# Row sums behind the first query tile, low keys in both halves, head 1's first loads inside the list, adaptive bias behind its weights

## The chip, the cores and the metric

The kernel runs on one core of one Trainium2 chip. The time is the device time of one launch in microseconds (us). TensorE (PE, with its weight loads PEld) multiplies matrices, VectorE (DVE) and ScalarE (ACT) work on elements, GpSimd (POOL) and SyncE (SP) issue most of the transfers (DMA), POOL also a few element operations. SP and POOL hand out their transfers in order, each from a list of its own.

## The reference

One layer of a streaming encoder for 1024 prompt rows and 32 sample rows (1056 together), width 1024, all in fp32:

```python
ada = silu(c) @ w_ada + b_ada        # shift1, scale1, gate1, shift2, scale2, gate2
h = rms_norm(x, g_pre_mix) * (1 + sc1) + sh1
q_lat, c_kv, k_r, q_b, k_b, v_b, g_a, g_b = split(h @ w_in)
o_a = multi-head latent attention (8 heads, chunk mask, softmax)
o_b = stick-breaking attention of q_b, k_b, v_b (8 heads of 64, strictly causal):
    z  = q k / 8
    sp = where(mask, softplus(z), 0); later = reverse_cumsum(sp) - sp
    a  = where(mask, exp(log_sigmoid(z) - later), 0);  o = a v
merged = sigmoid(g_a) * (o_A @ w_proj_a) + sigmoid(g_b) * (o_B @ w_proj_b)
x = x + gt1 * rms_norm(merged @ w_out)
x = x + gt2 * rms_norm(conv_ffn(rms_norm(x) * (1 + sc2) + sh2))
```

The new keys and values of the stick-breaking branch are outputs too, in their natural layout.

## The kernel before

Every fp32 product is made of three products of shorter numbers: each operand is split in a high half (`hi`, ACT, line 65) and a low half (`lo`, DVE, line 68), and PE adds high·high, high·low and low·high. A tile's weights come into a `wr` buffer by DMA, ACT writes `wh`, DVE `wl`, and then PE can start.

**The stage that makes queries, keys and values** (`stage_qkv`) computes 16 column tiles of `h @ w_in` with 128 columns each. The first three are made plainly (`mtile`): the query tile of heads 0 and 1 (its spill of high and low halves to DRAM is issued on POOL), the key tile of the same heads, and a tile of the query latents (written to DRAM as `l2d`). The other ten are made in five pairs by `pair(i, ta, tb, ua, ub)`: a scheme with seven block products in place of eight, of which five, w1·T2, w2·T1, w3·T3, w4·T4 and w5·B22, work on sums. The sums on the weights' side (lines 575, 576, 579, 580) are made by DVE in each pair, and each is then split by ACT and DVE (`half`). The sums on the rows' side, `T1` to `T4`, are made once from the normalised rows `F12`, `F22` in `fq` by the generator `sums()`: its first step makes T3 and T2 on DVE and ACT, its second T1, its third T4. `next(S)` runs a step; it stands once behind the latent tile and twice inside `pair`. `fq` is later the place of the pairs' results `ua`, `ub`.

What belongs to a finished tile is deferred to `after(kind, p, u)`, and a step of it is run by each `bg()` in the next pairs: for keys and values PE transposes the tile (`natural`, line 456), ACT copies it to a `nat` buffer (462), POOL writes it out (468), and for values DVE splits it into an `sg` buffer (473, 474) that POOL spills as `vd` (475). For a query tile `after` splits at once: ACT writes QH into an `sg` buffer, POOL spills `qh`, DVE makes the low half in place (488), POOL spills `ql`. There are two `sg` buffers, shared by QH, KH and V.

**The attention stage** (`stage_sb`, with buffers from `att_pools`) goes over four pairs of heads (p = 0 to 3), in each over two heads, and for each head over eight query tiles of 128 rows, two to a group: groups 0 to 3 of the list are head 0's, 4 to 7 head 1's. A token such as `S2.0a` is a step (here the score), the group, the tile in it, and a part of the row. For a head, `queries(p, h)` loads on SP: Q high, KH into both halves of a 128-partition tile, Q low into the other half of Q, and the low keys into one half of `KLz`, whose other half is set to zero once by POOL (line 1084). `score` is then two matmuls: KH·Q (1098) and KLz·Q (1099). The V load follows (1094). These tiles lie where the sums T were, and the `att` buffers where `fq` and the `qkv` buffers were, so their first use waits for the last reader there.

The order on PE, ACT and DVE in this stage is a list written by hand, `ORDER` (line 657), which begins `S0.0 S0.1 a0.0 S1.0 a0.1 e0.0 e0.1 l0.0 f1 f1 l0.1 x0.0`: `S` a score tile, `a`, `e`, `l` absolute value, exponential and logarithm on ACT, `x`, `c`, `d` steps on DVE, `E` the last exponential, `T`, `h`, `v`, `V` transposes and values, and `f` a step of other work that fills PE. The filling work is `gates()`: the gate columns of `h @ w_in` (lines 72 to 74), and between them steps of `ada_step`, in which PE multiplies `w_ada` row blocks (line 211). For each block of columns `ada_step` issues four loads of `b_ada` (207), then the `w_ada` loads (209). `then` holds work that is issued after a token of the list, by name. SP has at most eight transfers under way: the next one waits for the landing of the one eight before it.

Of the kernel before, what the change touches and what calls it, by code (L numbers as in the profile page):

```python
# [8 lines left out]
F32 = mybir.dt.float32  # L9
# [8 lines left out]
P = 128  # L18
D = 1024
KT = 8  # L20
TP = 1024
# [11 lines left out]
BIG = 1056  # L33
# [11 lines left out]
class K:  # L45
# [151 lines left out]
    def ada_step(self, n, pool, tp, late):  # L197


        nc, a = self.nc, self.a  # L200
        ps = self.bank("mm")
        for i, (v, k) in enumerate(self.ada_todo[:n]):
            if k == 0:
                self.acc = self.tl(tp, [P, 256], F32, "ada")
                for j in range(4):
                    c = v * D + j * 256
                    nc.sync.dma_start(self.acc[32 * j : 32 * j + 32], a["b_ada"][0, c : c + 256].partition_broadcast(32))
            w = self.tl(pool, [P, D], F32, "wr")
            nc.sync.dma_start(w, a["w_ada"][0, k * P : (k + 1) * P, v * D : (v + 1) * D])
            for j in range(4):  # L210
                nc.tensor.matmul(ps[32 * j : 32 * j + 32, :256], self.cT[:, k], w[:, j * 256 : j * 256 + 256],
                                 start=i == 0, stop=i == n - 1)
            if i < n - 1:
                yield
        acc = self.acc
        late.append(lambda: nc.vector.tensor_tensor(acc, acc, ps[:, :256], ALU.add))
        del self.ada_todo[:n]
        self.ada_sum = v if k == KT - 1 else None
        yield
# [195 lines left out]
    def stage_qkv(self):  # L415
# [63 lines left out]
        def after(kind, p, u):  # L479

            x = u[:, :TP]
            low = x.bitcast(F32R)
            if kind == "q":
                QH = sg()
                self.hi(QH, x, 0.125)
                nc.gpsimd.tensor_scalar(self.qsb[:, p], u[:, TP:T], 0.125, None, ALU.mult)
                spill("qh", p, QH)
                stt(low, x, 0.125, fl(QH), ALU.mult, ALU.subtract)
                spill("ql", p, low)
                return  # L490
            if kind == "k":
                KH = sg()
                self.hi(KH, x)
                nc.gpsimd.tensor_copy(self.ksb[:, p], u[:, TP:T])
                spill("kh", p, KH)
            for t0 in (0, 4, 8):
                natural(u, p, kind, t0)
                yield
            if kind == "k":
                self.lo(low, x, KH)  # L500
                spill("kl", p, low)
# [59 lines left out]
        S = sums()  # L561

        def pair(i, ta, tb, ua, ub):

            def plus(u, h, b, ps, q):
                add(u[:, HC * h + cs[b].start : HC * h + cs[b].stop], ps[:, : ns[b]], q[:, cs[b]], ALU.add)

            ra, rb = raws.pop(0)
            a0, a1 = half(ra[:, :512]), half(ra[:, 512:])
            X, Y = ([self.bank(g) for _ in range(2)] for g in ("mm", "s"))  # L570
            for ps, w, x in ((X, a0, B11), (Y, a1, B21)):
                for b in range(2):
                    prod(ps[b], b, w, x, True)
            s1a, s1b = S1[:, :512], S1[:, 512:]
            add(s1b, rb[:, :512], rb[:, 512:], ALU.add)
            add(s1a, s1b, ra[:, :512], ALU.subtract)
            w1, w2 = half(s1a), half(s1b)
            s2a, s2b = rb[:, :512], s1b
            add(s2a, ra[:, :512], rb[:, :512], ALU.subtract)
            add(s2b, ra[:, 512:], s1a, ALU.subtract)  # L580
            for b in range(2):
                nc.scalar.copy(Q1[:, cs[b]], X[b][:, : ns[b]])
            next(S, None)
            for b in range(2):
                plus(ua, 0, b, Y[b], Q1)
            bg(2)
            Z = [self.bank(g) for g in ("s", "pv")]
            for b in range(2):
                prod(X[b], b, w1, T2, False)
                nc.scalar.copy(Q2[:, cs[b]], X[b][:, : ns[b]])  # L590
            bg()
            for b in range(2):
                prod(Z[b], b, w2, T1, True)
            w3, w4 = half(s2a), half(rb[:, 512:])
            bg()
            for b in range(2):
                prod(X[b], b, w3, T3, False)
                nc.scalar.copy(Q3[:, cs[b]], X[b][:, : ns[b]])
                plus(ub, 1, b, Z[b], Q3)
            w5 = half(s2b)  # L600
            if i < 4:
                raws.append((raw(col(*pairs[i + 1][0])), raw(col(*pairs[i + 1][1]))))
            next(S, None)
            bg()
            for b in range(2):
                prod(X[b], b, w4, T4, False)
                nc.scalar.copy(ub[:, cs[b]], X[b][:, : ns[b]])
            bg(2)
            for b in range(2):
                prod(Z[b], b, w5, B22, False)  # L610
                plus(ua, 1, b, Z[b], Q2)
            for t, u in ((ta, ua), (tb, ub)):
                g = after(*t, u)
                if t[0] == "q":
                    next(g, None)
                else:
                    back.append(g)
# [13 lines left out]
        spill("qh", 0, QH)  # L631
        spill("ql", 0, QL)

        kf, lf = S0, Q0
        wh, wl = self.w_in_tile(672 + 512)
        for c0, n, ps in self.mtile(wh, wl, self.Hh, self.Hl, self.BLK, KT, "s"):
# [4 lines left out]
        for c0, n, ps in self.mtile(wh, wl, self.Hh, self.Hl, self.BLK, KT, "mm mm pv"):  # L641
            nc.scalar.copy(lf[:, c0 : c0 + n], ps[:, :n])
        nc.gpsimd.dma_start(self.l2d, lf)
        next(S)
        bg(4)
        for i, (ta, tb) in enumerate(pairs):
            pair(i, ta, tb, *U[i % 2 * 2 : i % 2 * 2 + 2])
# [395 lines left out]
    def att_pools(self):  # L1043
        nc = self.nc
        self.sm2 = self.At = self.tc.alloc_tile_pool(name="att", bufs=2, reuse_waits="tile")
        for g, w, n in (("o", 256, 2), ("big", BIG, 3)):
            for _ in range(n):
                self.tl(self.At, [P, w], F32, g)
        self.obd, self.oad = ([self.dr.tile([P, T], F32, name=f"{n}{k}") for k in range(4)] for n in ("ob", "oa"))
# [11 lines left out]
    def stage_sb(self):  # L1061
# [9 lines left out]
        def queries(p, h):  # L1071
# [6 lines left out]
            d(KH[h][o], "kh")  # L1078
            d(Q[h][o], "ql")
            d(self.KLz[h][r], "kl")  # L1080

        def first(h):
            V[h], self.KLz[h], Q[h], KH[h] = t(f"V{h}"), t(f"KL{h}"), t(f"Q{h}"), t(f"KH{h}")
            nc.gpsimd.memset(self.KLz[h][64 - 64 * h : 128 - 64 * h].bitcast(F32), 0.0)

        first(1)
        self.reset = S.tile([P, 512], BF16, name="reset")
# [1 line left out]
        nc.vector.tensor_scalar(self.reset[:, 383:511], self.idt, -1.0, 1.0, ALU.mult, ALU.add)  # L1089
        self.diagonals(S)  # L1090
        first(0)
        for h in range(2):
            queries(0, h)
            nc.sync.dma_start(V[h].bitcast(F32).rearrange("r (t d) -> r t d", t=8), self.vd[0][:, :, h])

        def score(h, ps, i, c0, n):
            q = slice(i * P, (i + 1) * P)
# [5 lines left out]
        for p in range(4):  # L1103
            then = {} if p == 3 else {"S3.1b": lambda: queries(p + 1, 0), "V3.0": lambda: values(p + 1, 0),
                                      "S7.1b": lambda: queries(p + 1, 1), "V7.0": lambda: values(p + 1, 1)}
            with self.tc.manual_schedule(engines={E.PE, E.Activation, E.DVE}):
                self.sb_attend(score, lambda b, h: V[h][:, b * P : b * P + P], self.store(self.obd[p]), fill, then)
        self.in_w.append(self.next_w.pop(0))
# [1442 lines left out]
```

## Time and profile before

| what | value |
| --- | --- |
| median of three runs | 1728.09 us (1727.78 to 1728.87) |
| the profiled execution, whole | 1731.74 us |
| its span, first to last instruction | 1729.9 us |
| instructions | 30270 |
| PE busy | 1669.2 us |
| DVE, ACT, POOL busy | 1273.2, 992.7, 294.6 us |
| PE's longest wait in the stretch of the list's start | 8.82 us |
| PE's longest wait in the first pair | 7.06 us |

The profile's page gives for each engine the busy time and number of instructions; the wait list gives for one engine what ended its idle time; the windows give busy times in stretches, with the granted clock of PE (1.00 is full) and what DMA moved. A timeline row is the start, the duration, the engine, the line, the operation, what is written from what, the shape, and, in brackets, the idle time before it with what ended it. Numbers in the order listings below are of another kind: they say which instruction stands behind which, and nothing of time.

### The profile page before, as it was taken

To read this page: it belongs to the slowest core of one execution; us is meant where nothing else is said; L and a number is where in the kernel's file an instruction comes from. 1 tells how busy PE (TensorE), PEld (TensorE's weight loads), DVE (VectorE), ACT (ScalarE), POOL (GpSimd) and SP (SyncE) were. 2 spreads that over 40 slices of the span, in tenths; PEclk is the share of its full clock that TensorE was granted. 3 is DMA by queue.
4 is the path that set the end of the run, shared out by engine and by line. 5 is a ranking of instruction groups with operands and counts; after the bars stand their busy time and mean duration, and the time that the engine had idled before them with its cause. 6 is when DMAs were issued, how large, how long until landed. Compare 5 with 4: busy or idle time off the path is not lost. (4 is left out here: it accounts for less than half of the span.)

```text
span 1729.9 us, 30270 instructions
## 1 busy us (share of the span) xinstructions
PE 1669.2 (96%) x11646; PEld 1518.2 (88%) x11646; DVE 1273.2 (74%) x2129; ACT 992.7 (57%) x1934; POOL 294.6 (17%) x566
## 2 busy tenths in 40 slices
PE   6979889999999999999999999999999999999997
PEld 3979879999999989988889789999999999977886
DVE  4485478879795577888675779887787787788456
ACT  4444368879795567777674276454444444545442
POOL 2113311111111131111000031211121111110013
PEclk8989989999999999999999999999999999999999
DMA  9325765565644241222165530523323333697643
GB/s 326 97 88 181 233 207 156 163 181 147 168 120 115 74 132 44 72 64 75 54 234 171 186 138 25 178 92 128 129 92 129 129 101 132 228 330 248 224 143 119
DMA packets 185343, 253.10 MB, mean 146 GB/s; under 512 B 14574, under 2 KB 125440, under 8 KB 185200
## 3 DMA queue, kind: packets, MB, share of 16 engines
q1 hardware_dynamic: 165072, 192.53, 35.9%
q0 software_dynamic: 19904, 58.56, 9.6%
q8 instruction: 91, 1.49, 0.4%
q14 instruction: 52, 0.43, 0.1%
q10 hardware_dynamic: 224, 0.09, 0.0%
HBM read 185.76 MB, written 64.57 MB: 145 GB/s over the span
## 5 line engine op out<-in xcount | busy, mean ns | idle before, releaser
L65 ACT ACTIVATE wh<-wr 128x1024 fp32r<-128x1024 f32 (+5 forms) x163 | 132.2, 820 | 228.9 <-PE s L2004 83.9
L68 DVE TENSOR_TENSOR wl<-wr,wh 128x1024 fp32r<-128x1024 f32 (+5 forms) x163 | 151.4, 937 | 90.4 <-ACT wh L65 90.3
L72 PE MATMUL mm<-hh,wh 128*128 128x352 f32 x456 | 155.3, 341 | 0.0
L73 PE MATMUL mm<-hl,wh 128*128 128x352 f32 x456 | 150.5, 330 | 0.2 <-DVE hl L302 0.2
L74 PE MATMUL mm<-hh,wl 128*128 128x352 f32 x456 | 149.6, 328 | 0.0
L2003 PE MATMUL mm<-T,wh 128*128 128x256 f32 (+1 forms) x376 | 109.5, 292 | 1.8 <-ACT wh L65 1.8
L2005 PE MATMUL mm<-T,wl 128*128 128x256 f32 (+1 forms) x376 | 108.0, 289 | 0.3 <-DVE wl L68 0.2
L2004 PE MATMUL mm<-T,wh 128*128 128x256 f32 (+1 forms) x376 | 108.3, 288 | 0.0
L2003 PE MATMUL s<-T,wh 128*128 128x256 f32 (+1 forms) x348 | 99.5, 286 | 7.1 <-ACT wh L65 7.1
L2005 PE MATMUL s<-T,wl 128*128 128x256 f32 (+1 forms) x348 | 99.2, 285 | 0.0
L2004 PE MATMUL s<-T,wh 128*128 128x256 f32 (+1 forms) x348 | 99.0, 284 | 0.0
L68 DVE TENSOR_TENSOR wl<-S,wh 128x1024 fp32r<-128x1024 f32 (+1 forms) x55 | 59.0, 1077 | 48.9 <-ACT wh L65 48.5
L72 PEld LDWEIGHTS mm<-hh,wh 128*128 128x128 f32 x456 | 87.4, 192 | 7.2 <-ACT o L755 3.3
L73 PEld LDWEIGHTS mm<-hl,wh 128*128 128x128 f32 x456 | 87.4, 192 | 3.2 <-DVE hl L302 1.7
L2144 DVE SCALAR_TENSOR_TENSOR u<-u,c,u 128x1058 f32<-128x1058 f32 x68 | 87.0, 1317 | 2.2 <-ACT u L2141 1.0
L74 PEld LDWEIGHTS mm<-hh,wl 128*128 128x128 f32 x456 | 87.4, 192 | 0.4 <-issue 0.3
L769 PE MATMUL tr<-c,A 128*128 128x128 f32 x576 | 84.1, 275 | 0.9 <-ACT A L728 0.3
L65 ACT ACTIVATE wh<-S 128x1024 fp32r<-128x1024 f32 (+1 forms) x55 | 51.6, 942 | 48.7 <-PE s L2004 13.1
L2005 PE MATMUL tr<-T,wl 128*128 128x272 f32 (+1 forms) x272 | 77.6, 285 | 0.1
L2003 PE MATMUL tr<-T,wh 128*128 128x272 f32 (+1 forms) x272 | 77.7, 286 | 0.0
L2004 PE MATMUL tr<-T,wh 128*128 128x272 f32 (+1 forms) x272 | 77.3, 284 | 0.0
L2003 PEld LDWEIGHTS mm<-T,wh 128*128 128x128 f32 x376 | 72.0, 191 | 3.9 <-ACT wh L65 3.3
(753 smaller groups left out, 5788.8 us busy)
## 6 DMA issues: line engine op xcount, KB each, us to landing
wr<-in_w_ada_dram SPq DMA_DIRECT2D x48, 512.0 KB, 5.0
wr<-in_w_up_dram SPq DMA_DIRECT2D x44, 512.0 KB, 3.9
dr<-in_w_down_dram SPq DMA_DIRECT2D x43, 512.0 KB, 5.9
wr<-in_w_in_dram SPq DMA_DIRECT2D x33, 512.0 KB, 4.8
wr<-gdn SPq DMA_DIRECT2D x30, 512.0 KB, 4.6
gdn<-u POOLq DMA_DIRECT2D x23, 512.0 KB, 4.9
gd<-nat POOLq DMA_DIRECT2D x48, 176.0 KB, 2.5
t<-gd SPq DMA_DIRECT2D x16, 528.0 KB, 4.7
```

The source lines that it names most:

```text
L65: self.nc.scalar.activation(out, in_, AF.Identity, scale=scale)
L68: return self.nc.vector.tensor_tensor(out, full, hi.bitcast(F32), ALU.subtract)
L72: m(ps, lh, rh, start=start, stop=False)
L73: m(ps, lh, rl, start=False, stop=False)
L74: self.pe = m(ps, ll, rh, start=False, stop=stop).ins
L769: self.nc.tensor.transpose(tr[:, (2 * s + q) * P : (2 * s + q + 1) * P], at[q][:, b * P : b * P + P], self.idt)
L2003: m(ps[:, :n], w[0][:, k], x[0][:, k, c], start=first and k == 0, stop=False, skip_group_check=True)
L2004: m(ps[:, :n], w[0][:, k], x[1][:, k, c], start=False, stop=False, skip_group_check=True)
L2005: i = m(ps[:, :n], w[1][:, k], x[0][:, k, c], start=False, stop=k == 3, skip_group_check=True)
L2144: nc.vector.scalar_tensor_tensor(y, u[:, w : w + YW], self.cvT[:, w, cc : cc + 1], y, ALU.mult, ALU.add)
```

## The change

The diff, with lines of context left out:

```diff
@@ ada_step
         for i, (v, k) in enumerate(self.ada_todo[:n]):
-            if k == 0:
-                self.acc = self.tl(tp, [P, 256], F32, "ada")
-                for j in range(4):
-                    c = v * D + j * 256
-                    nc.sync.dma_start(self.acc[32 * j : 32 * j + 32], a["b_ada"][0, c : c + 256].partition_broadcast(32))
             w = self.tl(pool, [P, D], F32, "wr")
             nc.sync.dma_start(w, a["w_ada"][0, k * P : (k + 1) * P, v * D : (v + 1) * D])
...
             if i < n - 1:
                 yield
+        if self.ada_todo[0][1] == 0:
+            self.acc = self.tl(tp, [P, 256], F32, "ada")
+            for j in range(4):
+                c = v * D + j * 256
+                nc.sync.dma_start(self.acc[32 * j : 32 * j + 32], a["b_ada"][0, c : c + 256].partition_broadcast(32))
@@ after
             if kind == "q":
-                QH = sg()
+                QH = sg() if p == 1 else flat(T1[0])[:, TP * (p - 2) : TP * (p - 1)]
                 self.hi(QH, x, 0.125)
@@ pair
             for b in range(2):
                 plus(ua, 0, b, Y[b], Q1)
-            bg(2)
+            bg()
             Z = [self.bank(g) for g in ("s", "pv")]
...
                 nc.scalar.copy(ub[:, cs[b]], X[b][:, : ns[b]])
-            bg(2)
+            bg()
             for b in range(2):
                 prod(Z[b], b, w5, B22, False)
                 plus(ua, 1, b, Z[b], Q2)
+            bg()
@@ stage_qkv
         spill("ql", 0, QL)
+        next(S)
         kf, lf = S0, Q0
...
         nc.gpsimd.dma_start(self.l2d, lf)
-        next(S)
         bg(4)
@@ att_pools
-        for g, w, n in (("o", 256, 2), ("big", BIG, 3)):
+        for g, w, n in (("o", 256, 2), ("big", BIG, 3), ("QZ", 256, 1), ("nat", 512, 2)):
@@ stage_sb
             d(self.KLz[h][r], "kl")
+            d(self.KLz[h][o], "kl")
 
         def first(h):
             V[h], self.KLz[h], Q[h], KH[h] = t(f"V{h}"), t(f"KL{h}"), t(f"Q{h}"), t(f"KH{h}")
-            nc.gpsimd.memset(self.KLz[h][64 - 64 * h : 128 - 64 * h].bitcast(F32), 0.0)
...
-        for h in range(2):
+
+        def begin(h):
             queries(0, h)
             nc.sync.dma_start(V[h].bitcast(F32).rearrange("r (t d) -> r t d", t=8), self.vd[0][:, :, h])
+
+        begin(0)
...
+            if p == 0:
+                then["S2.0a"] = lambda: begin(1)
```

So the first step of the row sums stands behind the first query tile's spills, and its temporaries no longer collide with the latents; QH of the last two query tiles (p = 2, 3) lies in T1's place; one `bg()` step in each of two places of a pair is put behind its last product; the low keys are loaded into both halves of `KLz` (eight more loads of 256 KB), so the second score matmul also adds low keys times low queries in place of zeros; head 1's first loads are issued after the token `S2.0a`; and the bias of an adaptive step is loaded behind the step's weights.

On DVE, around the first pair's first sums of results (`L566`; `T_...` are halves of the row sums, `S1` and `wr` the weights' sums, `wl` low halves, `nat` a transposed value tile, `sg` its split), there stood before:

```order
L575 TENSOR_TENSOR S1_525<-wr_148_726 128x512
L546 TENSOR_TENSOR fq_99<-fq_99 128x4x264
L68 TENSOR_TENSOR T_133_521<-fq_99,T_132_520 128x4x264
L576 TENSOR_TENSOR S1_525<-S1_525,wr_147_724 128x512
L68 TENSOR_TENSOR T_133_521<-fq_99,T_132_520 128x4x264
L68 TENSOR_TENSOR wl_163_914<-S1_525,wh_162_913 128x512 x2
L579 TENSOR_TENSOR wr_148_726<-wr_147_724,wr_148_726 128x512
L580 TENSOR_TENSOR S1_525<-wr_147_724,S1_525 128x512
L68 TENSOR_TENSOR T_131_519<-fq_99,T_130_518 128x4x264 x2
L566 TENSOR_TENSOR fq_99<-s_160_861,q1_529 128x256
```

and there stands now:

```order
L68 TENSOR_TENSOR T_131_519<-fq_99,T_130_518 128x4x264 x2
L555 TENSOR_TENSOR fq_99<-hh_16_94,fq_99 128x4x264 x2
L556 TENSOR_TENSOR fq_99<-fq_99,hl_17_95 128x4x264 x2
L68 TENSOR_TENSOR S1_525<-S1_525,sg_152_829 128x1024
L68 TENSOR_TENSOR T_127_515<-fq_99,T_126_514 128x4x264 x2
L566 TENSOR_TENSOR fq_99<-s_160_861,q1_529 128x256
L566 TENSOR_TENSOR fq_99<-s_161_862,q1_529 128x272
L473 COPY sg_181_1162<-nat_134_526 128x8x64
L575 TENSOR_TENSOR S1_525<-wr_148_748 128x512
L474 TENSOR_TENSOR sg_181_1162<-nat_134_526,sg_181_1162 128x8x64
```

All row sums now stand ahead of the pair's `L566`, and the weight sum `L575` stands behind `L566` and behind the cast of a transposed value tile.

On SP, where the first adaptive weights and the first heads' loads are issued (`Q0`, `KH0`, `KL0`, `V0` are head 0's tiles, `Q1` and so on head 1's; `wr` are weight buffers, `ada` the bias), there stood before, behind the first `w_ada` load:

```order
L1073 DMA Q0_283_2213<-qh0_533 64x1024
L1073 DMA KH0_284_2214<-kh0_541 64x1024 x2
L1073 DMA Q0_283_2213<-ql0_537 64x1024
L1073 DMA KL0_282_2212<-kl0_545 64x1024
L1094 DMA V0_281_2211<-vd0_549 128x8x128
L1073 DMA Q1_277_2201<-qh0_533 64x1024
L1073 DMA KH1_278_2202<-kh0_541 64x1024 x2
L1073 DMA Q1_277_2201<-ql0_537 64x1024
L1073 DMA KL1_276_2200<-kl0_545 64x1024
L1094 DMA V1_275_2199<-vd0_549 128x8x128
L207 DMA ada_292_2248<-in_b_ada_dram 32x256 x4
L209 DMA wr_294_2259<-in_w_ada_dram 128x1024
```

and there stands now, behind the same load:

```order
L204 DMA wr_294_2248<-in_w_ada_dram 128x1024
L1074 DMA Q0_284_2213<-qh0_533 64x1024
L1074 DMA KH0_285_2214<-kh0_541 64x1024 x2
L1074 DMA Q0_284_2213<-ql0_537 64x1024
L1074 DMA KL0_283_2212<-kl0_545 64x1024 x2
L1096 DMA V0_282_2211<-vd0_549 128x8x128
L214 DMA ada_295_2254<-in_b_ada_dram 32x256 x4
L82 DMA wr_296_2263<-in_w_in_dram 128x8x128
L1074 DMA Q1_278_2202<-qh0_533 64x1024
L1074 DMA KH1_279_2203<-kh0_541 64x1024 x2
```

The second `w_ada` load has moved from behind both heads' loads to ahead of them, head 0's low keys are loaded twice, and the bias, the next gate weights and then head 1's loads follow.

On POOL, at the end of the pairs, there stood before (`sg` is a split buffer, `T_130` half of T1):

```order
L652 DMA sbd_532<-sb_531 128x256
L449 DMA qh2_535<-sg_265_2153 128x1024
L449 DMA ql2_539<-fq_99 128x1024
L449 DMA qh3_536<-sg_266_2159 128x1024
L449 DMA ql3_540<-fq_99 128x1024
```

and there stands now:

```order
L449 DMA qh3_536<-T_130_518 128x1024
L475 DMA vd3_552<-sg_263_2118 128x1024
L468 DMA out_10_dram<-nat1_528 32x128
L477 COPY sb_531<-nat1_528 32x128
L486 TENSOR_SCALAR sb_531<-fq_99 128x32
L449 DMA qh2_535<-T_130_518 128x1024
L449 DMA ql2_539<-fq_99 128x1024
L449 DMA ql3_540<-fq_99 128x1024
L653 DMA sbd_532<-sb_531 128x256
```

The spills of the last two query tiles have moved ahead of the sample rows' transfers `sbd`, and one of them ahead of the last value spill.

## The prediction

> **What bounds the kernel now.** I read the page's first part, then TensorE's waits over the whole run, then windows of 3.41 us around the two largest of those that lie at the places the diff touches, and there the engines' timelines.
>
> ```profile
> PE 1669.2 (96%) x11646; PEld 1518.2 (88%) x11646; DVE 1273.2 (74%) x2129; ACT 992.7 (57%) x1934; POOL 294.6 (17%) x566
> ...
> PE mm L211 <- DMA wr<-in_w_ada_dram: 10.8, 4, 8.8
> PE s L2003 <- ACT wh L65: 7.4, 2, 7.1
> ```
>
> TensorE (PE) is busy for 96% of 1729.9 us, so only its idle time, or time at a lower granted clock, can be won. The wait list names one stop of 8.8 us and one of 7.1 us. Windows show both places and the stretch between them; the columns are the stretch, its length, the busy time of PE, weight load, DVE, ACT and POOL, the granted clock, the DMA share and GB/s.
>
> ```profile
> 87.07:90.48 3.41, 1.29 (x11) 1.07 (x9) 3.41 (x5) 0.48 (x2) 0.00 (x0) 1.00 0.32 126
> 90.48:93.89 3.41, 0.00 (x0) 0.00 (x0) 3.41 (x4) 2.07 (x3) 0.00 (x0) 0.50 0.00 0
> ...
> 100.72:104.13 3.41, 3.41 (x17) 3.28 (x15) 3.41 (x6) 0.79 (x3) 0.00 (x0) 0.50 0.59 150
> 104.13:107.55 3.42, 3.36 (x27) 3.21 (x27) 2.11 (x3) 0.34 (x2) 0.00 (x0) 1.00 0.39 83
> 105.00:208.00 103.00, 102.69 (x829) 100.23 (x829) 60.70 (x103) 45.08 (x93) 32.36 (x54) 1.00 0.55 172
> 207.50:219.00 11.50, 2.58 (x22) 1.64 (x20) 3.89 (x6) 2.11 (x2) 5.94 (x13) 0.75 1.07 339
> 230.43:233.84 3.41, 3.41 (x12) 3.18 (x13) 2.83 (x6) 2.70 (x7) 0.00 (x0) 0.50 0.65 226
> ```
>
> At 87 to 104 DVE is full and DMA idle: place A, set by DVE. From 105 to 208, the other four pairs, PE lacks 0.3 us. At 207.5 DMA carries 339 GB/s with PE at 2.58 of 11.5 us: place B. After each gap the clock is 0.50 for some windows (from 90.48 to 104.13, and again from 230.43), so a gap is paid for twice. The window at 87.07, in which PE was busy 1.29 of 3.41 us, is already followed by a slow one.
>
> **Part 1, the row sums (place A).** PE's and then DVE's and ACT's rows:
>
> ```profile
> 87.95 0.29 PE L2004 MATMUL s<-hl,wh 128*128 128x272 f32 x1
> 88.08 0.29 PE L2005 MATMUL s<-hh,wl 128*128 128x272 f32 x1
> 95.42 0.58 PE L2003 MATMUL s<-T,wh 128*128 128x256 f32 x1 [7.06 <-ACT wh L65]
> 97.99 0.58 PE L2003 MATMUL mm<-T,wh 128*128 128x256 f32 x1 [1.76 <-ACT wh L65]
> 98.37 0.42 PE L2004 MATMUL mm<-T,wh 128*128 128x256 f32 x1
> 98.59 0.43 PE L2003 MATMUL mm<-T,wh 128*128 128x272 f32 x1
> ...
> 70.38 0.69 DVE L68 TENSOR_TENSOR wl<-wr,wh 128x512 fp32r<-128x512 f32 x1 [5.94 <-ACT wh L65]
> 82.35 1.23 DVE L68 TENSOR_TENSOR S<-S,sg 128x1024 fp32r<-128x1024 f32 x1 [10.41 <-PE tr L456]
> 93.65 0.68 DVE L575 TENSOR_TENSOR S<-wr 128x512 f32<-128x512 f32 x1
> 109.05 0.42 DVE L566 TENSOR_TENSOR fq<-s,q 128x256 f32<-128x256 f32 x1 [0.31 <-ACT q L598]
> 117.46 0.42 DVE L473 CAST sg<-nat 128x512 fp32r<-128x512 f32 x1
> 94.75 0.61 ACT L65 ACTIVATE wh<-S 128x512 fp32r<-128x512 f32 x1
> 113.51 0.59 ACT L462 COPY nat<-tr 128x512 f32<-128x512 f32 x1 [1.75 <-PE tr L456]
> ```
>
> PE stops at 88.37 and starts at 95.42: the weight sum L575 stands behind the sums in DVE's order, runs at 93.65, then ACT splits it. PE's second stop is 1.76. Until the window from 104.13 the clock is 0.50: a matmul of 256 columns follows at 0.22 (98.37 to 98.59), where the full clock has 0.13 (87.95 to 88.08). From the resumption at 95.42 to 104.13 that is 8.7 us with 1.8 idle; some 6.9 us of work at half rate would take about 3.5 at full. Cost of place A: 7.06 + 1.76 + 3.4 = 12.2.
>
> With the sums behind the first query tile, DVE has its 5.94 and 10.41 us of idle for them, and the change's order puts every T sum ahead of pair 0's first L566. What is late next is a chain: last matmul 88.37, L566 on DVE 0.42 to 88.9, PE's transposes of `natural` to 89.5 (four; my estimate from the 0.13 pitch plus start-up), ACT's L462 0.59 to 90.1, DVE's cast L473 0.42 to 90.5, L575 0.68 to 91.2, ACT's split 0.61 to 91.9. PE resumes at 91.9, not 95.42. A second stop for the low half (a 0.69 row behind the split, with four matmuls in between) is about 0.7 against 1.76. Idle without the transposes: 3.1 + 0.7 = 3.8, against 8.8: 5.0 won, or 8.4 if the clock also stays at full (12.2 - 3.8). But the 3.5-us hole can leave a window as empty as the one at 87.07 was, and one window of 3.41 us at half then costs 1.7, two 3.4. The range is 5.0 to 8.4; I take one or a little more, **6.4**. If the sums made the latents' low weights late instead (L68 at 70.38, which now queue behind sums in the 5.94-us gap), PE would wait there; by my layout they are ready about 0.5 us before PE asks, the thinnest cover in this part.
>
> The Trainium skill speaks against a slow window here: its page "TensorE: Matmul & The Clock Gate", section "What's actually happening", throttles only after at least one idle window of about 3.4 us. By it this part gives the 8.4. The window at 87.07 speaks against that rule: 1.29 us of matmuls in it, and the next is slow.
>
> `bg()` steps are regrouped in pairs 1 to 4, whose PE lacks 0.3 us in 103: nothing, covered by DVE's 42 and ACT's 58 idle us there. If that cover failed, each late split would be one stop of about a row, 0.6.
>
> **Part 2, the loads (place B).** The rows of SP and DVE, PE, ACT and POOL, and the landings (KB, median us):
>
> ```profile
> 195.64 0.51 SPq L1073 DMA_DIRECT2D Q<-qh  x1
> 207.40 1.46 DVE L68 TENSOR_TENSOR wl<-wr,wh 128x1024 fp32r<-128x1024 f32 x1
> 208.26 0.28 PE L1098 MATMUL s<-KH,Q 128*128 128x256 f32 x1
> 210.58 0.39 PE L1099 MATMUL s<-KL,Q 128*128 128x256 f32 x1 [2.04 <-POOL KL L1084]
> 211.48 0.64 PE L211 MATMUL mm<-wr,cT 128*32 128x256 f32 x8
> 220.94 1.08 PE L211 MATMUL mm<-wr,cT 128*32 128x256 f32 x8 [8.82 <-DMA wr<-in_w_ada_dram]
> 221.96 0.66 PE L72 MATMUL mm<-hh,wh 128*128 128x352 f32 x1
> 226.23 0.49 PE L74 MATMUL mm<-hh,wl 128*128 128x352 f32 x1
> 214.21 1.06 ACT L65 ACTIVATE sg<-fq 128x1024 fp32r<-128x1024 f32 x1 [7.44 <-issue]
> 226.79 0.55 ACT L708 ACTIVATE A<-s 128x128 f32<-128x128 f32 x2 [8.68 <-DMA ql<-fq]
> 228.13 0.67 DVE L714 SCALAR_TENSOR_TENSOR A<-s,A 128x128 f32<-128x128 f32 x2 [8.49 <-ACT A L712]
> 230.31 0.66 PE L1098 MATMUL s<-KH,Q 128*128 128x512 f32 x1 [3.59 <-DVE A L726]
> 219.66 0.53 POOL L449 DMA_DIRECT2D ql<-fq  x1 [0.73 <-DVE QZ L952]
> KL<-kl SPq DMA_DIRECT2D x3, 256.0 KB, 7.5
> V<-vd SPq DMA_DIRECT2D x1, 512.0 KB, 12.3
> ql<-fq POOLq DMA_DIRECT2D x2, 512.0 KB, 6.9
> ```
>
> In this order S0.0 runs at 208.26 and 210.58, the first adaptive step at 211.48, then 8.82 us pass until the second one's weights. But what starts the attention is another thing: ACT's first absolute value (L708, 226.79) waits for the last ql spill, issued at 219.66 and landed 6.9 later; from there DVE and ACT pace PE to 230.31. So the arrival of the weights alone is worth nothing; both have to move.
>
> *Spills.* QH of pairs' p 2 and 3 no longer takes an `sg` buffer, so ACT does not stand 7.44 us before 214.21 for a buffer to come free; the last QL spill leaves at about 213.3 (6 us sooner) and lands at 220 to 222. ACT's L708 no longer waits for it at all: the preallocated QZ and nat tiles take that memory, and DVE's QZ memset waits in its place, right before L714. L714 at about 222.3, plus the 2.18 us from 228.13 to 230.31: the second scores may start at 224.5.
>
> *Loads.* The second w_ada load now stands ahead of all head-0 loads in SP's queue and waits for DVE's L68 of the gate weights, which read the buffer: 207.40 to 208.86 here, behind the two reset rows; these come later in the change's order, and I take 207.6 for its end. Queued behind it are Q twice, KH twice, KL twice and V: head 0 is issued from 208, not 195.64 as now. That is the loss. Up to the second KL it is 512 + 6 x 256 KB = 2.0 MB. At 339 GB/s alone that is 6.2 us (to 214.3); if as much of POOL's queue runs beside it (four Q spills of 512 KB), 12 us (to 220.5). I take 10: S0.0 at **218**, not 208.26. Then three pairs of scores, 1.0 us at full clock (from 210.58 to 211.48 and one more), 1.5 at half: 219.5. Two adaptive steps of 1.02 (220.94 to 221.96): 221.6. 15 fill matmuls took 4.8 at half clock (221.96 to 226.72); a clock that comes back midway makes 3.4: 225. Both roads meet there: the second scores at **225**, against 230.31, wins 5.3. PE then has no gap from 226.72 behind it, so the 3.41 us at half clock after 230.43 come at full: 1.7. Together **7.0**; with S0.0 at 220.5, 4.5; with QL landed at 220 and the loads early, 9.5.
>
> The Trainium skill, "DMA: Bandwidth & Descriptors", section "Issuing engines are not separate DMA queues", has transfers of SP and POOL interleave on the same 16 engines, so a load pushed into the spills' stretch is paid there. The trace agrees: 12.3 us for the V load that was issued when the last V spill and outputs left, against 7.5, KL's median.
>
> *The rest.* Eight more KL loads of 256 KB are 2 MB, 6 us of transfer at 339 GB/s in all; head 0's first is counted above, and the others have the attention on one head to land under (45 us, from 208 to 253). The KL memsets leave POOL, and with them the 2.04-us wait before 210.58; the 218 contains that already. Head 1's loads go out behind S2.0a, after 221, and are asked for by S4.0, which stands in the list behind the token S3.1b on which pair 1's loads hang; those go out now at:
>
> ```profile
> 253.31 0.59 SPq L1073 DMA_DIRECT2D KH<-kh  x1
> ```
>
> Even at 12.3 us of landing there are 15 to spare. b_ada behind its weights: four small loads, wanted only by a late add. Nothing, or up to 2.0 either way, what L211 waits in all beside its 8.8. I take off 0.4 for these.
>
> **Sum.** 6.4 + 7.0 - 0.4 = 13.0. The trace is one execution of 1731.74 us (span 1729.9, 1.84 around it), 3.65 above the median of 1728.09; I take these gaps for the same in the median run, so 1728.1 - 13 = **1715**. Ends: 5.0 + 4.5 gives 1718.6; 8.4 + 9.5 gives 1710.2; with the last term's bounds 1720 and 1708.6.
>
> **Rivals.**
> 1. *No gain at B.* The loads share worse than evenly or the fills stay at half clock, S1.1 stays near 230 and only A counts: 1721.7. For it: 12.3 us landings, and every load moved 12 us later. Against it: that takes KL landing at 223, 15 us after issue. Chance 0.17.
> 2. *The clock stays at full in place A*, because 3.5 us of gap straddle two windows and empty neither: gain 8.4 + 7.0 - 0.4 = 15, **1713**. Against: the window of 1.29 busy. Chance 0.15. The skill's clock rule named above gives the same time.
> 3. *The moved sums are not free*: they make the latents' weights late, PE stops there and gives back most of A, and with B at its low end 3 to 4 us are left: 1724.5. Chance 0.07, since 0.5 us of slack is little but the delay would have to reach 5.
> 4. *Slower.* SP's queue: head 0's loads behind the waiting w_ada load arrive so late that PE stands longer than before. It decides from the point where the second scores start after 230.3 + 6.4 = 236.7, that is KL landing after about 230, 22 us after issue. At 30 us the second scores start at 245, and the time is 8.3 over the median: 1736. Longest landing here: 12.3. Chance 0.05.
>
> **How the numbers follow.** Forecast 0.56, rivals 0.17, 0.15, 0.07, 0.05. The likeliest case gives 1710 to 1719.5; rivals 1 and 2 pull the range to 1709 to 1722, which leaves out rivals 3 and 4 and some tail, under 0.2. About 0.2%, 3.5 us, is what a measurement here can tell from no change. Faster by more: forecast and rivals 1 and 2, and half of 3: 0.90. Same: the rest of 3 and a little of 4: 0.06. Slower: 0.04.
>
> **What would show it.** Right: PE resumes near 92 after 88.4; the wait at L211 of 8.8 gone, a wait of L1098 or L1099 on head 0's loads until about 218 in its place; L714 behind ql near 222; the second scores near 225; the whole later part shifted by a constant. Wrong: a new PE wait near 71 on DVE's low weights; KL landing past 222; ACT's L708 still on ql; a wait of S4.0 on head 1.

## The result and the profile after

| | before | the change |
| --- | --- | --- |
| median (runs) | 1728.13 us (4) | 1717.48 us (4) |
| lowest to highest | 1727.78 to 1728.87 | 1715.79 to 1718.60 |
| profiled execution, whole / span | 1731.74 / 1729.9 | 1717.57 / 1715.8 |

The ratio is 0.9937, with a 95% interval of 0.9920 to 0.9954: 10.65 us faster by the medians, 14.2 by the two profiled executions. TensorE's waits over the whole run of the change, first three that matter (line waited for, then us in all, times, longest):

```profile
PE s L1102 <- DMA Q<-ql: 9.3, 1, 9.3
...
PE s L2009 <- ACT wh L65: 2.5, 1, 2.5
...
PE s L1103 <- DMA KL<-kl: 1.9, 1, 1.9
```

The 8.8-us wait for the second adaptive weights is gone and a 9.3-us wait for head 0's loads has taken its place; the 7.1-us wait of the first pair is 2.5. The windows of the change at the first pair:

```profile
87.07:90.48 3.41, 1.60 (x12) 1.12 (x10) 1.17 (x3) 0.58 (x1) 0.46 (x1) 1.00 0.49 184
90.48:93.89 3.41, 1.93 (x11) 1.71 (x12) 3.41 (x7) 2.37 (x4) 0.84 (x2) 0.92 0.56 201
93.89:97.31 3.42, 3.42 (x19) 3.42 (x19) 1.79 (x3) 0.41 (x2) 0.00 (x0) 0.58 0.59 165
97.31:100.72 3.41, 3.41 (x30) 3.41 (x29) 0.23 (x1) 1.28 (x3) 0.00 (x0) 1.00 0.67 172
```

DVE is full in one of these windows, where it was full from 87 to 104; DMA is no longer idle, and one half-clock window of 3.41 us is left in place of four. Place A and place B in the timelines of the change, TensorE, then the engines that feed it:

```profile
88.61 0.44 PE L456 MATMUL tr<-c,fq 128*128 128x128 f32 x2 [0.38 <-DVE fq L566]
91.58 0.39 PE L2009 MATMUL s<-T,wh 128*128 128x256 f32 x1 [2.52 <-ACT wh L65]
92.72 0.39 PE L2011 MATMUL s<-T,wl 128*128 128x256 f32 x1 [0.39 <-DVE wl L68]
...
210.08 0.58 PE L1102 MATMUL s<-KH,Q 128*128 128x256 f32 x1 [9.27 <-DMA Q<-ql]
212.56 0.55 PE L1103 MATMUL s<-KL,Q 128*128 128x256 f32 x1 [1.91 <-DMA KL<-kl]
214.11 1.94 PE L206 MATMUL mm<-wr,cT 128*32 128x256 f32 x16
215.98 0.54 PE L72 MATMUL mm<-hh,wh 128*128 128x352 f32 x1
218.59 0.39 PE L1102 MATMUL s<-KH,Q 128*128 128x512 f32 x1
...
199.56 0.34 SPq L204 DMA_DIRECT2D wr<-in_w_ada_dram  x1
200.00 0.51 SPq L1074 DMA_DIRECT2D Q<-qh  x1
204.94 1.05 POOL L449 DMA_DIRECT2D ql<-fq  x2 [0.66 <-DVE fq L488]
216.26 0.58 DVE L715 SCALAR_TENSOR_TENSOR A<-s,A 128x128 f32<-128x128 f32 x2
ql<-fq POOLq DMA_DIRECT2D x2, 512.0 KB, 10.0
```

The idle time of the first pair is 0.38 + 2.52 + 0.39 = 3.3 us. At the start of the attention TensorE waits from 200.8, runs the scores from 210.08 and 212.56, both adaptive steps together, and the fill, and has no wait left before the second scores at 218.59. DVE's L715 begins at 216.26, after the ql spills that were issued from 204.94 and took 10 us.

**Where the time came from.** All traces have 11646 matmuls, so they can be compared by number. The matmuls number 300, 640, 1200, 1500 and the last stand at 62.0, 122.1, 191.5, 250.0 and 1719.5 us in the first profile of before. What a kernel gains on that profile ahead of the first of them is its gain at the start, and between two of them at place A (the first pair), at "C" (pairs 1 to 4), at B (start of the attention), and in the rest. In the kernels with the earlier sums seven transposes have moved from ahead of number 640 to behind it, and seven products the other way, so A and C do not hold quite the same work in every row. Length is from the end of the last product or transpose to the second scores. All in us, with one profiled execution in each row:

| kernel | start | A | C | B | rest | length at B |
| --- | --- | --- | --- | --- | --- | --- |
| before, first profile | 0 | 0 | 0 | 0 | 0 | 21.9 |
| before, second profile | +1.8 | 0.0 | -3.7 | +3.3 | -0.5 | 20.2 |
| the change | +0.2 | +8.7 | -1.3 | +5.5 | +1.0 | 17.8 |
| the change, second profile | +1.6 | +8.6 | -1.9 | +4.5 | -1.5 | 19.0 |
| sums_only | +1.3 | +7.8 | -1.0 | +2.8 | +0.6 | 20.7 |
| no_sums | +1.4 | +1.1 | -8.2 | +3.9 | -0.5 | 17.8 |
| head0_manual | +1.6 | +8.0 | -4.8 | +4.7 | -19.6 | 16.6 |
| late_apart | +1.9 | +8.5 | +1.1 | +4.8 | +0.5 | 18.7 |
| no_sums_apart | -1.5 | +0.7 | +1.7 | +4.6 | -1.6 | 18.1 |
| kl_dve | -0.4 | +8.1 | -6.2 | +1.8 | +0.7 | 21.7 |
| late_ada_pool | +0.6 | +8.6 | +1.8 | +5.2 | +0.8 | 15.7 |
| late_qh_sg | +1.5 | +7.8 | +0.3 | -0.6 | +1.3 | 21.4 |
| late_kl_once | +1.9 | +8.5 | +0.6 | +4.2 | +2.2 | 19.3 |
| late_head1 | +1.8 | +8.3 | +1.8 | -3.8 | +0.8 | 19.3 |

Two things stand out. A is about 8.5, above the 6.4 of the sum, in nearly all kernels with the earlier sums. And C, which the prediction took for nothing, moves by up to 8 us, and by 3.7 between two executions of the same kernel.

### The profile page after: what moved, and what is told of

The parts are those of the page before. It is cut to its first block, busy times and chain, and to the rows that moved or that the text cites. A ratio compares the mean times of both kernels' runs of the same rounds, so it can differ in the third digit from the quotient of the medians.

```text
span 1715.8 us, 30290 instructions
## 1 busy us (share of the span) xinstructions
PE 1662.9 (97%) x11646; PEld 1514.0 (88%) x11646; DVE 1272.7 (74%) x2129; ACT 992.6 (58%) x1934; POOL 293.7 (17%) x564
## 5 line engine op out<-in xcount | busy, mean ns | idle before, releaser
L770 PEld LDWEIGHTS tr<-c,A 128*128 128x128 f32 x576 | 67.3, 141 | 7.7 <-DVE PTl L68 1.4
```

The costliest lines, as they stand in the source:

```text
L770: self.nc.tensor.transpose(tr[:, (2 * s + q) * P : (2 * s + q + 1) * P], at[q][:, b * P : b * P + P], self.idt)
```

## The experiments

Each series ran on one chip beside its own runs of the kernel before; their medians were 1729.09 (first four kernels), 1731.25 (next four) and 1730.15 (last four), so ratios are compared.

**The kernel before once more.** No edit.

> The kernel before, once more. Theory: the first profile of it was 3.65 us over the median because of where its half-clock windows fell (13.7 us of them at 25.6, 13.7 at 90.5, 13.7 at 213.4, 3.4 at 230.4), so another execution near 1728.1 has the same two waits of TensorE (7.1 for the split of the weight sum, 8.8 for the second adaptive weights) but one or two half-clock windows of 3.41 us fewer, each worth up to 1.7 us. Rival: the two waits themselves are shorter in a usual execution, by 3 us together, with the same windows. Ratio 1.000.

Ratio 1.0014 (1.0004 to 1.0025): against itself, so a difference of 0.14% between two series means nothing here. Its span is 1729.0, its half-clock windows start at 23.4, 91.7, 146.3 and 214.5 (10.2, 10.2, 6.8 and 13.7 us). Neither expectation held as written: there is one window less at A and B each, but two new ones from 146.3, in the pairs, and the wait for the second adaptive weights is 12.6 us in place of 8.8, with 0.7 behind it in place of 3.6. What stands there, in TensorE's timeline:

```profile
143.90 0.25 PE L159 MATMUL tr<-c,sg 44*128 44x44 f32 x1 [0.17 <-DMA sg<-in_conv_w_dram]
145.38 0.26 PE L159 MATMUL tr<-c,sg 44*128 44x44 f32 x1 [0.57 <-DMA sg<-in_conv_w_dram]
```

These transposes belong to `late_vectors`, nine small loads (norm weights, convolution weights) that POOL issues behind the first query pair; TensorE has their transposes right behind in its order. The first profile had no wait there; the change has one of 1.07 us.

**The sums alone.** The kernel before with one line moved (the loop that issues both heads' first loads is also written as two calls, in the same order):

```diff
         spill("ql", 0, QL)
+        next(S)
         kf, lf = S0, Q0
...
-        next(S)
         bg(4)
```

> The kernel before with only the row sums moved behind the first query tile. Theory (the two places add up): TensorE's stop in the first pair falls from 7.1 to about 2.5 us, place B keeps its 8.8-us wait, and the time is 1728.1 - 7.5 = 1720.6 (1719 to 1723). Rival (place B gives it back, since it waits for spills and loads that do not come earlier): 1725 or more.

1724.2 us, ratio 0.9964 (0.9951 to 0.9976): 6.2 us by the ratio, 4.9 by the two medians, less than the theory's 7.5 and more than the rival's 3. A gains 7.8. At B the old wait is even longer, since the second adaptive weights stay where they were in SP's queue:

```profile
214.31 1.08 PE L211 MATMUL mm<-wr,cT 128*32 128x256 f32 x8 [11.17 <-DMA wr<-in_w_ada_dram]
221.13 0.47 PE L1102 MATMUL s<-KH,Q 128*128 128x512 f32 x1 [1.26 <-DVE A L726]
```

**All but the sums.** The changed kernel with that line back:

```diff
-        next(S)
         kf, lf = S0, Q0
...
+        next(S)
         bg(4)
```

> The changed kernel with the row sums back behind the latent tile. Theory (add up): the 7-us stop in the first pair is back, the second scores start some 4 us earlier after the last product than before, one half-clock window less: 1728.1 - 5.8 = 1722.3 by the two traces, 1717.5 + 7.5 = 1725 by the medians. Rival (B's part is worth little without the earlier sums): 1727 to 1728.

1731.98, ratio 1.0016 (1.0005 to 1.0028), nothing gained: by its time the rival. But the table has B at +3.9, so it is not B that is worth nothing; C takes 8.2 back. TensorE stops for the late vectors, and half clock follows over 13.7 us of full work:

```profile
147.66 0.25 PE L159 MATMUL tr<-c,sg 13*128 13x13 f32 x1 [2.56 <-DMA sg<-in_g_kv_lat_dram]
...
150.00:155.00 5.00, 5.00 (x19) 3.63 (x19) 1.22 (x1) 0.97 (x2) 1.95 (x3) 0.50 0.30 96
155.00:160.00 5.00, 5.00 (x23) 4.62 (x23) 0.51 (x2) 0.66 (x2) 0.00 (x0) 0.50 0.38 140
```

**Head 0's loads first, SP in program order.**

```diff
-        begin(0)
...
-            with self.tc.manual_schedule(engines={E.PE, E.Activation, E.DVE}):
+            with self.tc.manual_schedule(engines={E.PE, E.Activation, E.DVE} | ({E.SP} if p == 0 else set())):
+                if p == 0:
+                    begin(0)
                 self.sb_attend(score, ...
```

> The changed kernel, with SP's order of the first pair of heads written down as the program has it, so that head 0's loads stand ahead of both adaptive weight loads. Theory (that position costs place B): the scores start at about 201 without the 9.3-us wait, the last ql spill lands 2 to 3 us sooner, the second scores start at about 215 in place of 218.6, and the time is 1714. Rival (the bytes have to pass anyway, and the ql spill and the second adaptive weights pace TensorE): the second scores at 218, 1717.

1739.59, ratio 1.0063 (1.0048 to 1.0078), slower, which neither expected. At B the theory's first half held: the scores start right behind the last product (203.38), and the length is 16.6. From there to the end 19.6 us are lost: between 250 and 330 TensorE waits 9.3 us in all for adaptive weights and 5.5 for DVE, with half-clock windows at 262.7 and 293.4, so the program's order on SP is a bad one for the rest of the list. That mixes two things, so the place in the queue was tried again in another way, below.

**The change once more.** No edit.

> The changed kernel, once more, beside the kernel before on this chip. Theory: 10 to 12 us under before; the first pair again 7 to 8 us shorter and the stretch from the last product to the second scores about 18 us against 20 to 22 of before. Rival (the stretch of the small late vectors, pair 1, differs between the two kernels and carries part of the difference): its loss is over 3 us in this execution, and the time moves with it.

1723.02, ratio 0.9953 (0.9940 to 0.9967), 8.2 us, under the theory's 10 to 12. A 8.6, length at B 19.0 (it has 13.7 us of half clock there, against 10.2 in the first profile), C -1.9 with two stops at the late vectors, under the rival's 3.

**The late vectors apart.** The changed kernel, with their loads issued behind pair 0 and the transposes left behind pair 1:

```diff
-            if i == 1:
-                self.late_vectors(sg().bitcast(F32))
+            if i == 0:
+                turn = self.late_vectors(sg().bitcast(F32))
+            if i == 1:
+                turn()
```

`late_vectors` only loads now, and returns `turn`, which makes the transposes and copies.

> The changed kernel, with the small loads of the late vectors issued behind pair 0 and their transposes left behind pair 1. Theory (TensorE stops there for these loads, 1 to 2.6 us, and sometimes trips the clock for 3 to 13 us): no wait of line 159's kind in the pairs, no half-clock window between 130 and 165, 1 to 4 us under the changed kernel. Rival (the staging buffer, held for a pair, stalls the value splits): the pairs get longer, time equal or above.

1716.86, ratio 0.9920 (0.9906 to 0.9933), 6 us under the changed kernel on the same chip and 14 under before: the theory, with more than it asked. No wait at the late vectors and no half clock in pairs 1 to 4; C is +1.1. The loads go out from 72.2 us here, from 134.7 in the change, and the seven transposes stand together. Of the 5.5 us between this profile and the second one of the change 3.0 are in C, 2.0 in the rest, which the edit does not touch. This is the version that beats both.

**The same without the sums.** On top of that edit:

```diff
-        next(S)
         kf, lf = S0, Q0
...
+        next(S)
         bg(4)
```

> The same without the earlier row sums. Theory (the changed kernel without the sums showed nothing, 1.0016, because a stop at the late vectors took back what the attention's start gained): 1725, 0.997 to 0.999 of before. Rival (the loads and spills are worth nothing by themselves): 1728 to 1731, ratio 1.000 or more.

1724.67, ratio 0.9962 (0.9949 to 0.9975): the theory, a little beyond it. With place C out of the way the loads and spills show their 4.6 at B, beside 1.7 at C; in no_sums they had shown nothing.

**Low keys once, zeros by DVE.**

```diff
-            d(self.KLz[h][o], "kl")
...
+            nc.vector.memset(self.KLz[h][64 - 64 * h : 128 - 64 * h].bitcast(F32), 0.0)
```

> The changed kernel with the low keys loaded once and the other half of the tile set to zero by DVE, which is idle there: 256 KB less ahead of the second score matmul, 2 MB less in all. Theory (the arrival of the loads at full DMA paces the start): low keys land 0.7 us sooner, the second scores start 0.5 to 1 us sooner, 1 us under the changed kernel. Rival (the last ql spill paces it): within 0.3 us of it.

1724.0, ratio 0.9959 (0.9943 to 0.9975), the time of the changed kernel on the same chip. Its profile fell badly at C (-6.2), and at B the second score matmul waits for the zeros, not for the keys:

```profile
221.38 0.58 PE L1103 MATMUL s<-KL,Q 128*128 128x256 f32 x1 [4.55 <-DVE KL L1085]
```

so what less traffic is worth does not show here.

**The second adaptive weights on POOL's queue**, on top of the late vectors apart:

```diff
-            nc.sync.dma_start(w, a["w_ada"][...])
+            (nc.gpsimd if (v, k) == (2, 1) else nc.sync).dma_start(w, a["w_ada"][...])
```

> The kernel with the late vectors apart, and the second adaptive weights of the first step loaded from POOL's queue, so that on SP head 0's loads no longer stand behind that load. Theory (head 0's place in SP's queue costs the 9.2-us wait before the first scores): no such wait, the first scores right behind the last product; the stretch from the last product to the second scores, about 18 us now, becomes 15 to 16.5, then paced by the last ql spill: 1 to 3 us under late_apart. Rival (the bytes pace it whatever their order): 17.5 or more, within 0.5 us of late_apart.

1716.25, ratio 0.9925 (0.9904 to 0.9945), the same as late_apart. The theory had the wait right and the time wrong: the scores start at 197.23 behind the last product, the length is 15.7 in place of 18.7, and nothing is won. TensorE and a window of this kernel:

```profile
197.23 0.36 PE L1113 MATMUL s<-KH,Q 128*128 128x256 f32 x1
202.67 1.08 PE L215 MATMUL mm<-wr,cT 128*32 128x256 f32 x8 [3.80 <-DMA wr<-in_w_ada_dram]
213.19 0.77 PE L1113 MATMUL s<-KH,Q 128*128 128x512 f32 x1 [4.74 <-DVE A L738]
...
215.00:220.00 5.00, 5.00 (x24) 5.00 (x23) 3.17 (x6) 3.83 (x10) 0.57 (x1) 0.63 1.10 227
```

The one long gap has become two, of 3.8 and 4.7 us. The second ends later, the clock goes to half at 211.9 for 6.8 us, and that lies over the work behind the second scores, while late_apart's half clock (13.7 us from 200.5) is over before its second scores at 215.65. Some 5.5 us of work at half rate cost 2.7, of the 3.0 gained.

**QH in the sg buffers again**, on top of the late vectors apart:

```diff
-                QH = sg() if p == 1 else flat(T1[0])[:, TP * (p - 2) : TP * (p - 1)]
+                QH = sg()
```

> The kernel with the late vectors apart, and QH of the last two query tiles in the sg buffers again. Theory (the place of QH is what frees the spills): the last ql spill leaves 4 to 6 us later, the absolute value's road sets the second scores, the stretch is 20 us or more, 2 to 4 us over late_apart. Rival (the loads' road paces it, and here head 0's loads stand ahead of the second adaptive weights again): 18 us or less, the time of late_apart.

1722.25, ratio 0.9952 (0.9936 to 0.9968), some 5 us over late_apart: the theory, and more. B falls from +4.8 to -0.6 and the length is 21.4, though head 0's loads are early here:

```profile
PE s L1113 <- DVE A L738: 11.0, 1, 11.0
...
207.96 0.53 POOL L458 DMA_DIRECT2D ql<-fq  x1 [0.73 <-DVE fq L497]
217.88 0.27 DVE L964 MEMSET QZ<- 128x256 f32 x1 [10.21 <-DMA ql<-fq]
```

The last ql spill leaves at 207.96, 9.1 us behind the last transpose; in late_apart, with QH in T1, it leaves at 201.61, 4.7 behind.

**Low keys once, zeros by POOL as before**, on top of the late vectors apart:

```diff
-            d(self.KLz[h][o], "kl")
...
+            nc.gpsimd.memset(self.KLz[h][64 - 64 * h : 128 - 64 * h].bitcast(F32), 0.0)
```

> The kernel with the late vectors apart, low keys loaded once, and the other half of their tile set to zero by POOL as before. Theory (POOL's queue reaches the second memset only behind the ql and sb spills): the second score matmul waits for POOL, by 0 to 2 us beyond its time now, and 2 MB less of loads bring nothing later: 0 to 2 us over late_apart. Rival (256 KB less ahead of the scores): 0.7 us under it.

1716.55, ratio 0.9923 (0.9904 to 0.9943): late_apart's time. The wait came as the theory said, and longer:

```profile
PE s L1113 <- DMA Q<-ql: 9.5, 1, 9.5
...
PE s L1114 <- POOL KL L1096: 3.4, 1, 3.4
```

but the length grows by 0.6 only. Neither the second low-key load nor its 2 MB can be seen in the time.

**Head 1's loads with head 0's**, on top of the late vectors apart:

```diff
         begin(0)
+        begin(1)
...
-            if p == 0:
-                then["S2.0a"] = lambda: begin(1)
```

> The kernel with the late vectors apart, and head 1's first loads issued with head 0's. Theory (they wait for the qh spills, with the bias and the next gate weights queued behind them, and share DMA with the ql spills): the stretch grows by 1 to 5 us, and the gate weights of the second step come late. Rival (SP is free there anyway): within 0.5 us of late_apart.

1725.39, ratio 0.9973 (0.9960 to 0.9985), 9 us over late_apart, more than the theory had. The profile has it at B, -3.8: SP stands before head 1's first load until 209.14, the bias and the gate weights follow, and the list stops later, for 6.47 us, until a step of DVE:

```profile
209.14 0.47 SPq L1085 DMA_DIRECT2D Q<-qh  x1
214.16 3.89 SPq L223 DMA_DIRECT2D ada<-in_b_ada_dram  x4
...
224.04 0.42 DVE L225 TENSOR_TENSOR ada<-ada,mm 128x256 f32<-128x256 f32 x1 [8.52 <-DMA ada<-in_b_ada_dram]
224.99 0.64 PE L1114 MATMUL s<-KH,Q 128*128 128x320 f32 x1 [6.47 <-DVE A L738]
```

That step, L738, stands in DVE's order behind L225, the add of the adaptive bias, and the add waits 8.52 us for the bias, which was issued at 214.16 behind head 1's loads (at 202.39 in late_apart, where the add waits for nothing).

## Why the prediction was right, and where it was off

**The time.** 1715 was forecast and 1717.48 measured, 13 against 10.65 us. The mechanism held at both places, but A came out 2.2 us above its term and B 3.6 below, and that they nearly cancel is luck. The means of the two profiles of each kernel give 12.2 us: A 8.6, B 3.4, C 0.2, and nothing at the start and in the rest.

**Place A, 6.4: under.** It measured 8.7 and 8.6 in two profiles of the change, 7.8 with the sums alone. The chain came as worked out: the last product ends at 88.37 in the trace before, TensorE resumes at 91.58 (91.9 forecast), and the idle time is 3.3 (3.8). "One or a little more" half-clock window was right too: one came, from 93.4 to 96.8, with TensorE busy all through it. The term that was too small is the idle time won. Over the whole of A it fell from 9.2 to 3.3 us, 5.9 where the sum had 5.0. The busy time at half clock fell from 6.95 to 3.41, worth 1.8 where the sum had 1.4. The last 1.0 is other busy time, of which every kernel with the earlier sums has less; the moved transposes may be part of it, and the cause stays open.

The regrouped `bg()` steps (by the diff two are taken out of a pair and one is put behind its last product, six in place of seven) show nothing at A, as the sum had it. The two variants without the sums gain 0.7 and 1.1 there, but their idle time is that of before, 9.4 us, and they are busy at half clock for 4.9 and 4.0 us in place of 6.95, which is the gain; the sums alone lack 0.9 with 5.7 us at half in place of 3.4. The low weights of the latents, the thinnest cover, held: DVE makes them at 69.15, and no wait of TensorE stands there.

**Place B, 7.0: over.** The matmul that needs the low keys started at 212.56, with the last product and transposes over at 200.8: 11.8 us, where the sum had 218 - 208.4 = 9.6. The ql spills took 10.0 us to land, where the sum had 6.7 to 8.7. So the second scores came 17.8 and 19.0 us after the last product, not 16.6; and the first profile of before, with 21.9, was a poor one for that place, where the second has 20.2. Measured within two profiles each, B is worth about 3.4 (the mean of 5.5 and 4.5, less half of 3.3), its length 21.05 - 18.4 = 2.7. Nearly all of it is idle time, 14.4 and 13.9 us before and 11.3 twice in the change: 2.9 where the sum had 5.3. The 1.7 of the clock is not shown: the busy time at half clock is 9.2 and 3.1 us before, 4.3 and 6.6 in the change.

The rate was the sum's: from the issue at 199.56 to 212.56 DMA carried 332 GB/s, more towards the end, as two windows of the change show:

```profile
206.80:210.20 3.40, 0.12 (x1) 0.13 (x1) 0.00 (x0) 0.00 (x0) 0.59 (x3) 0.50 1.03 393
210.20:213.60 3.40, 1.49 (x5) 1.23 (x6) 0.00 (x0) 0.30 (x2) 0.00 (x0) 0.50 1.04 409
```

What was short was the count of bytes: 13 us at 332 GB/s are 4.3 MB, the sum's 10 us at 339 are 3.4. V, the last value spill and all four Q spills now fall into the same 13 us, and loads and spills stretch each other. That agrees with the Trainium skill, "DMA: Bandwidth & Descriptors", section "Issuing engines are not separate DMA queues", and the sum had taken the ql spill's landing from the trace before (6.9), or little over it, in spite of it. The prediction's own sign of this, V's 12.3 us beside KL's 7.5, sets 512 KB beside 256; like beside like, head 0's V in the same trace, issued at 201.76, landed in 7.8.

**Which road sets B.** The prediction had both roads meeting at 225, the loads' and the spills', and in the first profile of the change they do meet:

```profile
216.08 0.27 DVE L953 MEMSET QZ<- 128x256 f32 x1 [10.58 <-PE mm L206]
217.92 0.62 DVE L727 TENSOR_TENSOR A<-s,A 128x128 f32<-128x128 f32 x2
```

The QZ memset begins 0.2 us behind the landing of the last ql spill (215.87), as it does in late_apart (212.35 and 212.15); DVE's steps behind it end at 218.54, and TensorE comes to the second scores at 218.59 without a wait. Later spills lose: with QH back in the `sg` buffers all of B's gain is gone (0.9952 against 0.9920), though the loads are then early. Earlier loads alone (late_ada_pool) shorten the stretch by 3.0, until TensorE stops for DVE behind the spills, and the time by nothing that can be measured. "That is the loss", said of head 0's late issue, is true of the wait; of the time it is not shown.

**The rest, -0.4.** The second low-key load and the memset cost the same to within what is measured. Head 1's loads inside the list were costed at nothing, and are; but issued with head 0's they make the time 9 us worse, since SP then stands for the qh spills and DVE for the bias behind them. So the bias, "wanted only by a late add", costs nothing in the change because it is issued ahead of head 1's loads; behind them, in late_head1, it stops the list. Its place behind the weights alone was not tried.

**Pairs 1 to 4, nothing: its reason failed.** As a difference nothing shows: C is -1.6 for the change and -1.8 for before as means of two profiles, and the two of before lie 3.7 apart. But "PE lacks 0.3 us" was true of the one trace shown. The late vectors' loads lay just under TensorE's reach in it: the load that landed at 146.36 was transposed at 146.41. They stopped the change for 1.1 and 1.8 us, the second profile of before for 0.7 with 6.8 us of half clock behind it, and no_sums for 2.6 with 13.7. The prediction did not list them, neither in the sum nor among its rivals.

**The median.** "I take these gaps for the same in the median run" does not hold to 3 us. The profiled execution of before was 3.65 over its median, that of the change 0.1 over its own, and 14.2 - 10.65 is that difference. The half-clock windows that fall in different places in each execution are its likely cause, as far as two profiles can show it. The sum's outer ends, 1720 and 1708.6, should be 1720.6 and 1708.2 by its own 2.0; nothing rests on them.

**Rivals.** No gain at B: not so, but the 3.4 of B lies midway between it and the forecast. The clock at full in place A: the size is right (8.4), its reason is not, since one window came. The sums not free and the slower one: no sign of either.

## What to carry to other kernels

Before a stretch is costed at nothing because its wait is small, look at what ends just in time in it: here nine small loads ahead of seven transposes were within a microsecond of stopping TensorE, and issuing them earlier, with the transposes together, took 6 us off the changed kernel. Compare two kernels' traces matmul by matmul, and take two profiles of the kernel before: the difference between executions of one kernel was 3 us at each of two places. Where several transfers pace a start, time each by its landing in the crowd, and try the roads one by one; where two roads meet, making one of them shorter moves the wait and its half clock, not the end.

## What was not expected of the hardware

The granted clock goes to half without an idle window. In the change the longest gap near 90 is 2.52 us and TensorE is busy for 1.60 and 1.93 of two neighbouring windows of 3.41 us, and half clock follows from 93.4 to 96.8; in no_sums one stop of 2.56 us between full stretches was followed by 13.7 us of half clock with TensorE busy throughout (5.00 of 5.00 at 0.50, twice). In before_again two stops of 0.17 and 0.57 us were enough, in a window with TensorE busy for 2.67 of 3.41 us:

```profile
142.85:146.26 3.41, 2.67 (x17) 1.88 (x15) 1.64 (x3) 1.48 (x3) 1.36 (x4) 1.00 0.95 312
146.26:149.67 3.41, 3.41 (x13) 2.60 (x14) 0.00 (x0) 0.26 (x1) 0.78 (x1) 0.50 0.71 189
```

The Trainium skill, "TensorE: Matmul & The Clock Gate", section "What's actually happening", has at least one idle window before the throttle, and at least one busy window before the release. The traces have no idle window in these three places; the release came after one busy window in the change and after four in no_sums. The stop of 2.56 us there thus cost some 9 us, itself and half of 13.5 us of work; the table has 8.2 against before.
